# Expert stage without GpSimd arithmetic: splits on VectorE, the gate factor at the combine

## The chip, the cores and the metric

The kernel runs on one core of a Trainium2 chip. The metric is the device time of one execution in microseconds (us), the median of several runs. The engines are TensorE (PE, with its weight loads as PEld), VectorE (DVE), ScalarE (ACT), GpSimd (POOL) and SyncE (SP), whose queue issues the large loads.

## The reference, cut to what matters

Two transformer blocks on 512 tokens of width 1024, in fp32. The first has a delta rule and a sliding window, then a mixture of 32 experts of which each token takes 4; the second has attention, a recurrent layer and two MLPs. The change lies in the experts:

```python
logits = xf @ w_router + b_router
top_val, top_idx = lax.top_k(logits, 4)
gates = softmax(top_val)
# for the tokens of expert e:
hu = xb @ w_up[e] + b_up[e]                       # 1024 -> 2048
act = x_glu * sigmoid(1.702 * x_glu) * (x_lin + 1)  # both halves clipped at 7
ys = (act @ w_down[e] + b_down[e]) * row_gate     # summed by token
x = x + gate2 * moe(h)                            # gate2: one factor per column
```

## The kernel before, in words

Every fp32 weight block is turned into two parts whose products PE can take: `split` (L278 to L287) lets ACT write the rounded part `wh` (L281) and then DVE (L286) or POOL (L284) the rest, `wl = raw - wh`. `mm3` makes three products of the parts (L290 to L292), `prod` the like for blocks of 64 rows (L1168 to L1174).

Expert stage: the routing ranks the experts by their tokens. The list `units` holds 13 units of 256 rows, blocks of 128 or 64 rows of an expert. `gather_T` collects the rows of a unit by products with one-hot columns (`hot_cols`, L1083). An expert has twelve weight blocks of 128x2048, eight in `expert_up` and four in `expert_down`, each a load of 1 MB on SP's queue into one of six buffers `raw`. The list `pools` says which of the twelve POOL splits: blocks 4 and 2, more in the first unit. `expert_up` has the activation on ACT and DVE (L1204 to L1212), `split_T` the transposes. `expert_down` of an expert follows `expert_up` of the next; `expert_out` multiplies its rows by the routing gate on ACT or DVE, and its `finish` multiplies them on POOL by `g2bc`, the factor gate2 of the columns (L1262), and scatters them to `y_d` in DRAM by an indirect DMA of POOL (L1263). The buffer `yb` for this is single. `slots` (L1100 to L1111) makes the row numbers and gates of a block from a small product with the records `R`: four columns, put together by operations on one column each. The rows of the last two blocks don't pass through `y_d`: `add_rows` makes factors of a product from them (L1279 to L1281).

Combine: each token block of 128 takes the four slots of its tokens from `y_d` (`load_y`, L1550) and adds them to the residual `xs`, one addition in two on POOL (`add_ys`, L1554, L1555), and the products of the last blocks (L1573). The loads for the third and fourth token block follow the first loads of the attention's weights. Then the second block begins.

The order of each engine's instructions is not that of the source: the program is built with `schedule_with_timeline_sim=True`, which plans it from data dependences and assumed durations. An engine executes its own list in order. Of memory, a tile waits until the tile whose place it takes is no longer read.

Of the kernel before, what the change touches and what calls it, by code (L numbers as in the profile page):

```python
# [7 lines left out]
F = mybir.dt.float32  # L8
# [8 lines left out]
T = 512  # L17
# [5 lines left out]
SMALL = 18  # the experts by rank: from 2 up to 192 tokens for two of them, 64 from this one on, else 128  # L23
# [38 lines left out]
_RC, _NRC = _layout([("iota", 128), ("Us", 128), ("thi", 4), ("tlo", 4), ("p32", 1), ("d32", 1), ("eq", 32), ("kc", 32), ("cap", 32)])  # L62


def _rconst():
    import numpy as np
    c = np.zeros((128, _NRC), np.float32)

    def put(name, a):
        o, n = _RC[name]  # L70
        c[:, o:o + n] = a
    i = np.arange(128)
    put("iota", np.repeat(i[None], 128, 0))
    put("Us", i[:, None] < i[None])
    put("thi", np.arange(4)[None] * 8 + (i // 16)[:, None] - 32)
    put("tlo", np.repeat((i % 16)[:, None], 4, 1))
# [151 lines left out]
def tile_block(ctx, tc, A, out, dbg=None):  # L228
# [23 lines left out]
    # eight banks of PSUM, in groups that are used in turn  # L252
# [83 lines left out]
    def gemv(src, cofs, gp, bufs):  # L336
        """silu(c) @ src; columns 256 q .. 256 q + 255 end up in row 32 q"""
# [9 lines left out]
    def gemv_split(src, cofs, gp, ring_raw, nv=4):  # L347
        """the same, with the products and most of the sums on the other engines"""
# [35 lines left out]
    def mod_row(i, src, cofs, gp, bias, plus=0.0, mul=None, how="split"):  # L384
        """row i of md_d: (silu(c) @ src + bias + plus) * mul"""
# [82 lines left out]
    # gains and biases of the second block's norms, times sqrt(2) for the residual  # L468
# [33 lines left out]
    # gates of the delta rule  # L502
# [54 lines left out]
    def front(p):  # L557
        """doubled silu of the convolutions, inverse norms, the triangular systems"""
# [181 lines left out]
    # sliding-window attention; the logits of a head are kept in units of its slope  # L740
# [89 lines left out]
    # row slot * T + token of y_d; the last two experts' first tokens, of the slots 2 and 3, do not pass through it  # L830
# [11 lines left out]
    # output projection: the columns of the window's attention first  # L842
# [29 lines left out]
    # gated norm of the delta rule's output  # L872
# [29 lines left out]
    # residual, second norm, router  # L902
# [14 lines left out]
    # the norm's gain goes into the router's weights; the shift's share of the logits  # L917
# [18 lines left out]
    # those that are read last come first, away from the room of the experts' weights  # L936
# [7 lines left out]
    M = Z[:, :, 0:32]  # a token's chosen experts; then its gates, then its places  # L944
# [21 lines left out]
    # the experts' input bias in two parts, the columns' second half 64 rows further on  # L966
# [9 lines left out]
    def half_out(tb, ps, half):  # L976
        """half the columns of the residual, their share of its square and, before the norm's factor, of the logits"""
# [56 lines left out]
    # routing  # L1034
# [12 lines left out]
    thi = RC("thi").unsqueeze(2).to_broadcast([128, 4, 32])  # L1047
    R = mt([128, 4, 32, 4], "R")
    pool.memset(R[:, :, :, 3], 1.0)
    vec.tensor_copy(out=R[:, :, :, 1], in_=RC("tlo").unsqueeze(2).to_broadcast([128, 4, 32]))  # L1050

    # one plus a pair's place among its expert's tokens, 0 for the pairs that are not chosen
# [10 lines left out]
    # units of 256 rows; a block of rows is an expert's rank, its columns in the unit, and the places that it leaves out  # L1063
# [53 lines left out]
    def gather_T(hot, X, runs):  # L1117
        """hi and lo of the transposed rows of h2 that the one-hot columns select"""
# [14 lines left out]
    def rows_in(X, blk):  # L1133
        """the stationary operands of a block in X: hi, lo, and both side by side"""
# [44 lines left out]
    def expert_up(wsrc, bsel, rows, get=fetch):  # L1179
        """an expert's activations, in chunks of 256 of its hidden columns"""  # L1180
        acts_ = [mt([128, 1024], "ma", 2, F, mo)[0:r[0]] for r in rows]
        for j in range(4):
# [9 lines left out]
            for kh in range(2):  # L1192
                h, l = get(wsrc, 2 * j + kh, pool if 2 * j + kh in pools[0] else None)
# [21 lines left out]
    def split_T(src, to=None):  # L1215
        """the stationary operands of the transposed activations"""
# [28 lines left out]
    def gated(yb, y, gc, s):  # L1245
        """gate times 64 rows in two parts"""
# [4 lines left out]
    def expert_out(y, sl, r, yb=None):  # L1251
        """gates a block's rows; the function that it returns writes them to y_d"""
# [8 lines left out]
        def finish():  # L1261
            pool.tensor_tensor(out=yb[0:r], in0=yb[0:r], in1=g2bc[0:r], op=OP.mult)  # L1262
# [26 lines left out]
    def block_rows(blk):  # L1289
        """a block's one-hot columns, its rows of y_d and its gates"""  # L1290
# [7 lines left out]
    def ranked(rank):  # L1298
        """the weights and the bias of the expert of a rank"""
# [5 lines left out]
    def further_block(at, hot):  # L1305
# [7 lines left out]
        Rc, bs = mt([128, 4, 4], "Rc"), mt([128, 1], "bs", 1, FR)  # L1313
# [41 lines left out]
    vec.tensor_copy(out=R[:, :, :, 2], in_=z4[:, :, 32:64])  # L1355
# [16 lines left out]
    vec.scalar_tensor_tensor(out=R[:, :, :, 0], in0=jv.rearrange("p (t e) -> p t e", t=4), scalar=32.0, in1=thi,  # L1372
# [8 lines left out]
    def lists():  # L1381
        """the blocks beyond the experts' own: ranks, experts, offsets of their places, and the number of them"""
# [9 lines left out]
        # a block per partition: its rank is the number of ranks whose blocks all come before it  # L1392
# [4 lines left out]
        # places less 128 times the blocks before in the expert, less what its own hold  # L1397
# [23 lines left out]
    # experts  # L1421
# [3 lines left out]
    def begin(src, ready, ahead):  # L1425
        """the first weights of a block from what was loaded before"""
        def get(s, k, eng=None):
            if s is not src or k >= len(ahead):
                return fetch(s, k, eng)
# [3 lines left out]
            return msplit(ahead[k], eng)  # L1433
# [4 lines left out]
    def expert_bias():  # L1438
        # the residual, and the experts' output bias: hi * hi + lo * hi + hi * lo in one product
# [15 lines left out]
        for tb in range(NTB):  # L1455
# [18 lines left out]
    LOOP = 1  # the unit after which any further blocks come  # L1474
# [3 lines left out]
    for u, unit in enumerate(units):  # L1478
# [35 lines left out]
        if u == LOOP:  # L1514
            # any further blocks
# [584 lines left out]
```

## Time and profile before

| | |
|---|---|
| median of 3 runs | 3288.72 us (3272.14 to 3291.38) |
| profiled execution, span | 3273.7 us, 37859 instructions |
| PE busy | 2902.4 us, 89% |
| DVE busy | 2627.4 us, 80% |
| ACT busy | 1597.7 us, 49% |
| POOL busy | 1181.6 us, 36% |
| mean granted clock of PE | 0.947 |

The span goes from the first to the last instruction; no other time of the profiled execution is listed, and it lies within 2 us of the fastest of the runs. Busy time is that in which an instruction of the engine is open, waiting for a resource inside the instruction included. A row names the line, the engine, the operation, out<-in by the program's names and the form (partitions x elements), then the count; what stands after the second bar is idle time before the group and what ended it.

### The profile page before, as it was taken

How to read it: one execution, taken by the hardware profiler on the slowest of the kernel's cores; microseconds unless marked ns; L12 is line 12 of the kernel's file. 1: busy time of each engine (PE TensorE's matmuls, PEld its weight loads, DVE VectorE, ACT ScalarE, POOL GpSimd, SP SyncE). 2: the span in 40 equal slices, each digit the busy share in tenths (PEclk: the TensorE clock that was granted, in tenths of full speed). 3: DMA queues.
4: the chain of work that ended last, by engine and by line, in shares of the span. 5: the costliest groups of instructions: out<-in, count | busy, mean ns of one | idle time of the engine just before them, and what ended most of it. 6: DMA issues, size and time to landing. Idle time of an engine off the chain costs nothing.

```text
span 3273.7 us, 37859 instructions
## 1 busy us (share of the span) xinstructions
PE 2902.4 (89%) x13632; PEld 2225.4 (68%) x13632; DVE 2627.4 (80%) x3392; ACT 1597.7 (49%) x1960; POOL 1181.6 (36%) x531
## 2 busy tenths in 40 slices
PE   6889988888899898999989759889999889889997
PEld 4667866655677566667667537577777767678886
DVE  5986479989999999999998985686756888875456
ACT  4433344666666656666666544442223645533231
POOL 2330165334443343344434562233323243442223
PEclk9999979989999999999999879989999999989999
DMA  7552346778688778778878754345532322223321
GB/s 264 182 176 87 106 169 236 296 274 314 248 305 304 287 290 303 280 271 302 305 284 311 276 195 161 116 147 199 178 128 89 112 63 92 83 84 100 100 92 56
DMA packets 127201, 643.73 MB, mean 197 GB/s; under 512 B 17142, under 2 KB 18122, under 8 KB 77856
## 3 DMA queue, kind: packets, MB, share of 16 engines
q1 hardware_dynamic: 122064, 632.27, 53.8%
q0 software_dynamic: 4800, 8.46, 0.7%
q8 instruction: 109, 1.79, 0.2%
q14 instruction: 84, 0.69, 0.1%
q10 hardware_dynamic: 144, 0.52, 0.0%
HBM read 624.42 MB, written 21.59 MB: 197 GB/s over the span
## 4 chain that ended last, share of the span: by engine, by line
PE 38%; DVE 26%; issue 7%; ACT 4%; DMA 2%; POOL 1%; DVEq 0%; ACTq 0%; SPq 0%; POOLq 0%
DVE wl L286 9%; PE bank_d L290 4%; PE bank_d L292 4%; PE bank_d L291 4%; PE bank_u L290 3%; PE bank_u L292 3%; PE bank_u L291 3%; DVE ma L1211 3%; ACT wh L281 2%; PE bank_hu L290 2%; PE bank_hu L291 2%; PE bank_hu L292 1%; DVE ma L1208 1%; PE bank_tr L1125 1%; PE bank_hu L1173 1%
## 5 line engine op out<-in xcount | busy, mean ns | idle before, releaser
L281 ACT CAST wh<-raw 128x2048 fp32r<-128x2048 f32 (+1 forms) x615 | 958.0, 1579 | 528.5 <-PE bank_u L291 177.7
L286 DVE TENSOR_TENSOR wl<-raw,wh 128x2048 fp32r<-128x2048 f32 (+2 forms) x521 | 1065.1, 2052 | 149.0 <-ACT wh L281 147.0
L284 POOL TENSOR_TENSOR wl<-raw,wh 128x2048 fp32r<-128x2048 f32 (+1 forms) x94 | 443.0, 4715 | 659.8 <-ACT wh L281 603.1
L1682 POOL TENSOR_TENSOR h2h<-h2h,yt 128x512 f32<-128x512 f32 x161 | 237.5, 1482 | 679.5 <-DVE yt L1681 669.5
L1681 DVE TENSOR_TENSOR yt<-bank_d,G 128x512 f32<-128x512 f32 x168 | 113.2, 686 | 182.9 <-PE bank_d L292 180.1
L291 PE MATMUL bank_u<-h_lo,wh 128*128 128x512 f32 (+1 forms) x680 | 251.3, 370 | 9.8 <-DVE h_lo L1666 9.8
L290 PE MATMUL bank_u<-h_hi,wh 128*128 128x512 f32 (+1 forms) x680 | 252.2, 373 | 6.3 <-ACT wh L281 3.2
L292 PE MATMUL bank_u<-h_hi,wl 128*128 128x512 f32 (+1 forms) x680 | 251.6, 371 | 0.0
L291 PE MATMUL bank_hu<-wl,xT 128*128 128x512 f32 x576 | 236.2, 411 | 14.9 <-DVE wl L286 9.6
L290 PE MATMUL bank_hu<-wh,xT 128*128 128x512 f32 x576 | 233.5, 410 | 0.0
L292 PE MATMUL bank_hu<-wh,xT 128*128 128x512 f32 x576 | 231.4, 403 | 0.0
L1262 POOL TENSOR_TENSOR yb<-yb,g2bc 128x1024 f32<-128x1024 f32 (+1 forms) x32 | 108.9, 3404 | 282.3 <-ACT yb L1259 201.8
L1173 PE MATMUL bank_hu<-wl,xT 128*64 128x512 f32 x448 | 191.2, 427 | 21.0 <-DVE wl L286 20.6
L290 PE MATMUL bank_d<-wh,a 128*128 128x512 f32 x512 | 202.5, 396 | 5.6 <-DVE yt L1681 3.5
L291 PE MATMUL bank_d<-wl,a 128*128 128x512 f32 x512 | 200.9, 393 | 0.0
L292 PE MATMUL bank_d<-wh,b 128*128 128x512 f32 x512 | 197.5, 392 | 0.0
L1174 PE MATMUL bank_hu<-wh,xT 128*128 128x512 f32 x448 | 188.5, 421 | 0.0
L1209 ACT ACTIVATE mb<-ma 128x256 f32<-128x256 f32 (+1 forms) x136 | 56.6, 417 | 265.4 <-DVE ma L1208 245.0
L1211 DVE SCALAR_TENSOR_TENSOR ma<-mb,ma 128x256 f32<-128x256 f32 (+1 forms) x136 | 153.6, 1129 | 8.4 <-ACT mb L1209 8.2
L291 PEld LDWEIGHTS bank_u<-h_lo,wh 128*128 128x128 f32 x680 | 130.8, 192 | 32.5 <-DVE h_lo L1666 10.5
L290 PEld LDWEIGHTS bank_u<-h_hi,wh 128*128 128x128 f32 x680 | 130.6, 193 | 28.4 <-ACT wh L281 3.6
L292 PEld LDWEIGHTS bank_u<-h_hi,wl 128*128 128x128 f32 x680 | 130.7, 192 | 22.3
(626 smaller groups left out, 6572.5 us busy)
## 6 DMA issues: line engine op xcount, KB each, us to landing
raw<-in_w_up_dram SPq DMA_DIRECT2D x256, 1024.0 KB, 4.9
raw<-in_w_down_dram SPq DMA_DIRECT2D x128, 1024.0 KB, 5.1
raw<-in_mlp_w_dram SPq DMA_DIRECT2D x128, 512.0 KB, 4.4
graw<-in_ada_w_dram SPq DMA_DIRECT2D x72, 512.0 KB, 4.1
graw<-in_w_ada_dram SPq DMA_DIRECT2D x48, 512.0 KB, 4.6
raw<-in_ada_w_dram SPq DMA_DIRECT2D x24, 512.0 KB, 4.2
raw<-in_rnn_w_in_dram SPq DMA_DIRECT2D x24, 512.0 KB, 3.8
raw<-in_w_in_dram SPq DMA_DIRECT2D x22, 512.0 KB, 4.2
```

The lines of the kernel that those rows point to most:

```text
L281: act.copy(out=h, in_=r)
L284: pool.tensor_tensor(out=l, in0=r, in1=h.bitcast(F), op=OP.subtract)
L286: vec.tensor_tensor(out=l, in0=r, in1=h.bitcast(F), op=OP.subtract)
L290: pe.matmul(out=o, lhsT=lhs[0], rhs=rhs[0], start=first, stop=False)
L291: pe.matmul(out=o, lhsT=lhs[0], rhs=rhs[1], start=False, stop=False)
L292: pe.matmul(out=o, lhsT=lhs[1], rhs=rhs[0], start=False, stop=last)
L1173: pe.matmul(out=o[0:64], lhsT=hi(k), rhs=w[1], start=False, stop=False)
L1174: pe.matmul(out=o, lhsT=both(k), rhs=w[0], start=False, stop=last)
L1211: vec.scalar_tensor_tensor(out=a, in0=b, scalar=1.0, in1=a, op0=OP.add, op1=OP.mult)
L1262: pool.tensor_tensor(out=yb[0:r], in0=yb[0:r], in1=g2bc[0:r], op=OP.mult)
L1681: vec.tensor_tensor(out=t, in0=ps, in1=G[:, cs], op=OP.mult)
L1682: eng.tensor_tensor(out=xs[tb][:, cs], in0=xs[tb][:, cs], in1=t, op=OP.add)
```

## The change

In the expert stage POOL does no splits any more: all are DVE's. The factor gate2 is left out of `finish` and `add_rows`; the sum of a token's rows is multiplied by it once, at the combine, where all additions are DVE's. The records `R` have two columns instead of four (row number with its offset, half the gate), so `slots` needs two operations on the product instead of six. The one-hot columns of the four token blocks are made by one comparison with broadcast operands. The additions of the experts' output bias to the residual go to DVE. The loads of `y_d` for the second to fourth token block go into the six `raw` buffers, ahead of the attention's weights. Comments are removed too, which moves lines. Of the diff, cut to its core:

```diff
-    R = mt([128, 4, 32, 4], "R")
+    R = mt([128, 4, 32, 2], "R")
...
     def hot_cols(pos, hot):
-        for tb in range(NTB):
-            vec.tensor_scalar(out=hot[tb], in0=iob[:, 0:hot[tb].shape[1]], scalar1=pos[:, tb:tb + 1], scalar2=None,
-                              op0=OP.is_equal)
-        return hot
+        n = hot.shape[2]
+        vec.tensor_tensor(out=hot, in0=iob[:, 0:n].unsqueeze(1).to_broadcast([128, 4, n]),
+                          in1=pos.unsqueeze(2).to_broadcast([128, 4, n]), op=OP.is_equal)
+        return [hot[:, tb, :] for tb in range(NTB)]
...
     def slots(hot, Rsel):
-                pe.matmul(out=pt[o:o + n, 0:4], lhsT=hot[tb].bitcast(F), rhs=Rsel(tb), start=tb == 0, stop=tb == NTB - 1)
-        rec = mt([128, 4], "rec", 2)
-        vec.tensor_copy(out=rec, in_=pt[:, 0:4])
-        iv = mt([128, 1], "iv", 2)
-        vec.scalar_tensor_tensor(out=iv, in0=rec[:, 0:1], scalar=16.0, in1=rec[:, 1:2], op0=OP.mult, op1=OP.add)
-        pad = mt([128, 1], "pad", 2)
-        vec.tensor_scalar(out=pad, in0=rec[:, 3:4], scalar1=-8192.0, scalar2=8192.0, op0=OP.mult, op1=OP.add)
-        vec.tensor_tensor(out=iv, in0=iv, in1=pad, op=OP.add)
+                pe.matmul(out=pt[o:o + n, 0:2], lhsT=hot[tb].bitcast(F), rhs=Rsel(tb), start=tb == 0, stop=tb == NTB - 1)
         ii = mt([128, 1], "ii", 10, I32)
-        vec.tensor_copy(out=ii, in_=iv)
+        vec.tensor_scalar(out=ii, in0=pt[:, 0:1], scalar1=8192.0, scalar2=None, op0=OP.add)
         gc = mt([128, 1], "gc", 10)
-        vec.tensor_scalar(out=gc, in0=rec[:, 2:3], scalar1=0.5, scalar2=None, op0=OP.mult)
+        vec.tensor_copy(out=gc, in_=pt[:, 1:2])
...
-    pools = [(4,), (2,)]
...
-                h, l = get(wsrc, 2 * j + kh, pool if 2 * j + kh in pools[0] else None)
+                h, l = get(wsrc, 2 * j + kh)
...
-            h, l = get(wsrc, k2, pool if k2 in pools[1] else None)
+            h, l = get(wsrc, k2)
...
         def finish():
-            pool.tensor_tensor(out=yb[0:r], in0=yb[0:r], in1=g2bc[0:r], op=OP.mult)
             pool.indirect_dma_start(out=y_d, out_offset=bass.IndirectOffsetOnAxis(ap=sl[0][0:r, 0:1], axis=0),
...
     def add_rows(y, gc, hot, tiles):
-            vec.scalar_tensor_tensor(out=t, in0=y[h], scalar=gc, in1=g2bc[:, hs], op0=OP.mult, op1=OP.mult)
+            act.activation(out=t, in_=y[h], func=AF.Copy, scale=gc)
...
-    ready = {k: msplit(ahead[k], pool) for k in range(2)}
+    ready = {k: msplit(ahead[k]) for k in range(2)}
...
     def expert_bias():
-            pool.tensor_tensor(out=xs[tb], in0=xs[tb], in1=bt, op=OP.add)
+            vec.tensor_tensor(out=xs[tb], in0=xs[tb], in1=bt, op=OP.add)
...
-        pools[:] = [(1, 3, 5, 7), (0, 2)] if u == 0 else [(4,), (2,)]
-        if not nxt:
-            pools[1] = (0,)
...
-    def add_ys(y, tb):
-        for j in (0, 2):
-            pool.tensor_tensor(out=y[j], in0=y[j], in1=y[j + 1], op=OP.add)
-            vec.tensor_tensor(out=xs[tb], in0=xs[tb], in1=y[j], op=OP.add)
+    def sum_y(y):
+        for a, b in ((0, 1), (2, 3), (0, 2)):
+            vec.tensor_tensor(out=y[a], in0=y[a], in1=y[b], op=OP.add)
...
-    load_y(ys[1], 1)
-    add_ys(ys[0], 0)
+    for tb in range(1, NTB):
+        for j in range(2):
+            r = m_raw.tile([128, 2048], F, tag="raw", name="raw")
+            ys[tb] += [r[:, 0:1024], r[:, 1024:2048]]
+        load_y(ys[tb], tb)
+    sum_y(ys[0])
...
     for tb in range(NTB):
+        if tb:
+            sum_y(ys[tb])
         for h in range(2):
...
-            vec.tensor_tensor(out=xs[tb][:, hs], in0=xs[tb][:, hs], in1=o, op=OP.add)
-    add_ys(ys[1], 1)
+            vec.tensor_tensor(out=ys[tb][0][:, hs], in0=o, in1=ys[tb][0][:, hs], op=OP.add)
+        vec.tensor_tensor(out=ys[tb][0], in0=ys[tb][0], in1=g2bc, op=OP.mult)
+        vec.tensor_tensor(out=xs[tb], in0=xs[tb], in1=ys[tb][0], op=OP.add)
...
-    for tb in range(2, NTB):
-        load_y(ys[tb], tb)
...
-    for tb in range(2, NTB):
-        add_ys(ys[tb], tb)
```

## Rows read from the trace of the kernel before

**Rows 1.** Busy time by stretch: PE, PEld, DVE, ACT, POOL, clock, DMA share, GB/s
```profile
...
460.00:510.00 50.00, 37.08 (x197) 31.71 (x196) 37.85 (x54) 21.87 (x18) 33.48 (x7) 0.87 0.57 214
510.00:1860.00 1350.00, 1203.20 (x5473) 881.72 (x5473) 1281.06 (x1400) 843.29 (x747) 552.31 (x132) 0.95 0.78 288
```

**Rows 2.** Chain that ended last, 510 to 1860 us, by line
```profile
by line: DVE wl L286 17.0%; issue 13.1%; DVE ma L1211 6.6%; PE bank_hu L290 3.9%; PE bank_hu L291 3.7%; PE bank_hu L292 3.6%; DVE ma L1208 3.2%; PE bank_tr L1125 2.7%; PE bank_hu L1173 2.6%; PE bank_hu L1174 2.5%; PE bank_y L291 2.5%; PE ba
```

**Rows 3.** DVE's groups by form, 510 to 1860 us: busy us, mean ns, idle before
```profile
...
L286 DVE TENSOR_TENSOR wl<-raw,wh 128x2048 fp32r<-128x2048 f32 x297 | 724.0, 2445 | 31.8 <-ACT wh L281 31.5
L1211 DVE SCALAR_TENSOR_TENSOR ma<-mb,ma 128x256 f32<-128x256 f32 x71 | 88.6, 1248 | 0.9 <-ACT mb L1209 0.7
L1211 DVE SCALAR_TENSOR_TENSOR ma<-mb,ma 64x256 f32<-64x256 f32 x60 | 62.9, 1049 | 6.9 <-ACT mb L1209 6.8
L1208 DVE TENSOR_SCALAR ma<-ft 64x256 f32<-64x256 f32 x60 | 58.6, 976 | 0.3
L1212 DVE SCALAR_TENSOR_TENSOR ma<-ft,ma 64x256 f32<-64x256 f32 x60 | 52.1, 869 | 0.4
...
L1104 DVE SCALAR_TENSOR_TENSOR iv<-rec 128x1 f32<-128x1 f32 x34 | 36.6, 1075 | 0.2
...
L1083 DVE TENSOR_SCALAR hot<-iob,posm 128x128 fp32r<-128x128 bf16 x64 | 27.3, 486 | 0.0
L1107 DVE TENSOR_TENSOR iv<-iv,pad 128x1 f32<-128x1 f32 x34 | 26.6, 783 | 0.0
...
L1106 DVE TENSOR_SCALAR pad<-rec 128x1 f32<-128x1 f32 x34 | 4.8, 140 | 0.0
```

**Rows 4.** Single durations in that stretch: shortest, median, longest in ns
```profile
...
L286 DVE TENSOR_TENSOR wl<-raw,wh x297: 2268/2276/6474, 514.2 to 1857.6; 128x2048 fp32r<-128x2048 f32 x149
...
L1211 DVE SCALAR_TENSOR_TENSOR ma<-mb,ma x131: 402/409/5491, 512.0 to 1854.8; 128x256 f32<-128x256 f32 x71, 64x256 f32<-64x256 f32 x60
...
L1208 DVE TENSOR_SCALAR ma<-bank_hu x69: 402/410/425, 516.4 to 1789.8; 128x256 f32<-128x256 f32 x69
L1208 DVE TENSOR_SCALAR ma<-ft x60: 271/276/4610, 628.7 to 1852.2; 64x256 f32<-64x256 f32 x60
```

**Rows 5.** Order of time: POOL and DVE side by side, start and us
```profile
...
866.69 4.61 POOL L284 TENSOR_TENSOR wl<-raw,wh 128x2048 fp32r<-128x2048 f32 x1 [23.09 <-ACT wh L281]
...
866.96 4.62 DVE L1211 SCALAR_TENSOR_TENSOR ma<-mb,ma 64x256 f32<-64x256 f32 x1 [2.53 <-ACT mb L1209]
...
1432.84 5.88 POOL L1263 DMA_INDIRECT y_d<-yb,ii  x1 [0.28 <-POOL yb L1262]
...
1432.84 2.27 DVE L286 TENSOR_TENSOR wl<-raw,wh 128x2048 fp32r<-128x2048 f32 x1
```

**Rows 6.** POOL's groups by form, 510 to 1860 us
```profile
...
L284 POOL TENSOR_TENSOR wl<-raw,wh 128x2048 fp32r<-128x2048 f32 x63 | 336.8, 5347 | 489.4 <-ACT wh L281 438.1 <-DVE wl L286 18.1 <-DVE ma L1211 16.7
L1263 POOL DMA_INDIRECT y_d<-yb,ii x31 | 88.3, 2850 | 11.3 <-POOL yb L1262 7.3 <-issue 3.0 <-DVE ma L1212 0.6
L1262 POOL TENSOR_TENSOR yb<-yb,g2bc 128x1024 f32<-128x1024 f32 x18 | 57.6, 3202 | 201.8 <-ACT yb L1259 201.8
```

**Rows 7.** Order of time: two DVE operations, each alone
```profile
...
461.29 0.69 DVE L1341 TENSOR_TENSOR oh<-oh,gt 128x512 f32<-128x512 f32 x1
...
1944.66 1.21 DVE L1555 TENSOR_TENSOR h2h<-h2h,raw 128x1024 f32<-128x1024 f32 x1
```

**Rows 8.** Sums of L286, L281 over 52 stretches without POOL arithmetic; L281, 510:1860
```profile
...
sum 716.10, DVE 483.18; mean DVE 9.29
...
sum 716.10, ACT 383.45; mean ACT 7.37
...
sum 1350.00, ACT 677.62; mean ACT 677.62
```

**Rows 9.** DVE's groups by form, 1860 to 1960 us
```profile
...
L1555 DVE TENSOR_TENSOR h2h<-h2h,y 128x1024 f32<-128x1024 f32 x4 | 9.7, 2437 | 0.0
```

**Rows 10.** SP's queue, 1915 to 1940 us
```profile
...
1928.21 11.34 SPq L272 DMA_DIRECT2D raw<-in_attn_w_in_dram  x3
```

More of the change, by code (lines that the diff above doesn't have):

```diff
@@ L59, in _consts @@
     return c
-_RC, _NRC = _layout([("iota", 128), ("Us", 128), ("thi", 4), ("tlo", 4), ("p32", 1), ("d32", 1), ("eq", 32), ("kc", 32), ("cap", 32)])
+_RC, _NRC = _layout([("iota", 128), ("Us", 128), ("tok", 4), ("p32", 1), ("d32", 1), ("eq", 32), ("kc", 32), ("cap", 32)])
 def _rconst():
@@ L74, in _rconst @@
     put("Us", i[:, None] < i[None])
-    put("thi", np.arange(4)[None] * 8 + (i // 16)[:, None] - 32)
-    put("tlo", np.repeat((i % 16)[:, None], 4, 1))
+    put("tok", np.arange(4)[None] * 128 + i[:, None] - 512 - 8192)
     e = np.arange(32)
@@ L1046, in tile_block @@
     vec.tensor_scalar(out=iob, in0=RC("iota"), scalar1=1.0, scalar2=None, op0=OP.add)
-    thi = RC("thi").unsqueeze(2).to_broadcast([128, 4, 32])
-    R = mt([128, 4, 32, 4], "R")
-    pool.memset(R[:, :, :, 3], 1.0)
-    vec.tensor_copy(out=R[:, :, :, 1], in_=RC("tlo").unsqueeze(2).to_broadcast([128, 4, 32]))
+    tok = RC("tok").unsqueeze(2).to_broadcast([128, 4, 32])
+    R = mt([128, 4, 32, 2], "R")
     pp = trbank()
@@ L1080, in hot_cols @@
     def hot_cols(pos, hot):
-        for tb in range(NTB):
-            vec.tensor_scalar(out=hot[tb], in0=iob[:, 0:hot[tb].shape[1]], scalar1=pos[:, tb:tb + 1], scalar2=None,
-                              op0=OP.is_equal)
-        return hot
+        n = hot.shape[2]
+        vec.tensor_tensor(out=hot, in0=iob[:, 0:n].unsqueeze(1).to_broadcast([128, 4, n]),
+                          in1=pos.unsqueeze(2).to_broadcast([128, 4, n]), op=OP.is_equal)
+        return [hot[:, tb, :] for tb in range(NTB)]
     def hot_of(blk):
-        return [hots[-1][:, tb, blk[1]:blk[1] + blk[2]] for tb in range(NTB)]
+        return hots[-1][:, :, blk[1]:blk[1] + blk[2]]
     hot_unit()
@@ L1149, in tile_block, with msplit, fetch @@
     turn = [0]
-    def msplit(r, eng=None):
+    def msplit(r):
         ring[1:3] = rings[turn[0] % 2]
         turn[0] += 1
-        return split(r, eng)
-    def fetch(src, k, eng=None):
-        return msplit(raw(src(k)), eng)
-    pools = [(4,), (2,)]
+        return split(r)
+    def fetch(src, k):
+        return msplit(raw(src(k)))
     def prod(o, rows, k, w, first, last, then=None):
@@ L1273, in add_rows @@
             for o in (0, 64):
-                pe.matmul(out=pt[o:o + 64, tbs[tb]], lhsT=hot[tb].bitcast(F), rhs=ident, start=True, stop=True)
+                pe.matmul(out=pt[o:o + 64, tbs[tb]], lhsT=hot[:, tb, :].bitcast(F), rhs=ident, start=True, stop=True)
         act.copy(out=hotT, in_=pt)
@@ L1354, in tile_block @@
     vec.tensor_copy(out=M2, in_=z4[:, :, 0:32])
-    vec.tensor_copy(out=R[:, :, :, 2], in_=z4[:, :, 32:64])
+    vec.tensor_scalar(out=R[:, :, :, 1], in0=z4[:, :, 32:64], scalar1=0.5, scalar2=None, op0=OP.mult)
     vec.tensor_copy(out=posm, in_=z4[:, :, 64:96])
@@ L1370, in tile_block @@
                            op0=OP.mult, op1=OP.add)
-    vec.scalar_tensor_tensor(out=R[:, :, :, 0], in0=jv.rearrange("p (t e) -> p t e", t=4), scalar=32.0, in1=thi,
+    vec.scalar_tensor_tensor(out=R[:, :, :, 0], in0=jv.rearrange("p (t e) -> p t e", t=4), scalar=512.0, in1=tok,
                              op0=OP.mult, op1=OP.add)
@@ L1425, in begin, with get @@
     def begin(src, ready, ahead):
-        def get(s, k, eng=None):
+        def get(s, k):
             if s is not src or k >= len(ahead):
-                return fetch(s, k, eng)
+                return fetch(s, k)
             if k in ready:
@@ L1432, in get @@
                 return ready[k]
-            return msplit(ahead[k], eng)
+            return msplit(ahead[k])
         return get
@@ L1523, in tile_block, with loop_fetch @@
             lr = [mt([128, 1024], "aT", 3, F, mo) for _ in range(2)]
-            def loop_fetch(src, k, eng=None):
+            def loop_fetch(src, k):
                 for b, r in enumerate(lr):
@@ L1534, in tile_block @@
                 hot = mt([128, 1024], "ma", 2, FR, mo)[:, 0:512].rearrange("p (t s) -> p t s", t=4)
+                sl, wu_, wd_, bs = further_block(ds(i_, 1), hot)
                 hot = [hot[:, tb, :] for tb in range(NTB)]
-                sl, wu_, wd_, bs = further_block(ds(i_, 1), hot)
                 xd, ad = (t.rearrange("p (k c) -> p k c", k=8) for t in lx)
@@ L1550, in load_y @@
             sync.dma_start(out=t, in_=y_d[j * T + tb * 128:j * T + tb * 128 + 128, :])
-    def add_ys(y, tb):
-        for j in (0, 2):
-            pool.tensor_tensor(out=y[j], in0=y[j], in1=y[j + 1], op=OP.add)
-            vec.tensor_tensor(out=xs[tb], in0=xs[tb], in1=y[j], op=OP.add)
-    ys = [[h2_("l", j) for j in range(4)], []]
-    load_y(ys[0], 0)
-    for j in range(2):
-        r = m_raw.tile([128, 2048], F, tag="raw", name="raw")
-        ys[1] += [r[:, 0:1024], r[:, 1024:2048]]
-    load_y(ys[1], 1)
-    add_ys(ys[0], 0)
+    def sum_y(y):
+        for a, b in ((0, 1), (2, 3), (0, 2)):
+            vec.tensor_tensor(out=y[a], in0=y[a], in1=y[b], op=OP.add)
+    ys = [[h2_("l", j) for j in range(4)]] + [[] for tb in range(1, NTB)]
+    load_y(ys[0], 0)
+    for tb in range(1, NTB):
[4 more added lines that the diff above has]
+    sum_y(ys[0])
     aT = [mt([128, 8, 128], "aT", 3, FR, mo).rearrange("p a b -> p (a b)") for _ in range(2)]
@@ L1598, in tile_block @@
     sm = tc.alloc_tile_pool(name="sm", bufs=1, reuse_waits="tile")
-    yp = tc.alloc_tile_pool(name="yp", bufs=1, reuse_waits="tile")
-    ys += [[yp.tile([128, 1024], F, tag="y", name="y", bufs=8) for j in range(4)] for tb in range(2, NTB)]
     first = []
```

3 lines of the change are left out of this document (1 added, 2 removed).

## Prediction

> **What bounds the kernel now.** The span is 3273.7 us. I first cut it into stages, by the view of busy time per stretch [rows 1]. In the expert stage, 510 to 1860 us, VectorE (DVE) is busy 1281.06 of 1350 us, 94.9%; TensorE (PE) 1203.20, ScalarE (ACT) 843.29, GpSimd (POOL) 552.31. Then the chain that ended last, in that stretch [rows 2]: its largest shares are DVE's splits (L286, 17.0%) and a small product of the activation (L1211, 6.6%), which is worth looking at because 256 columns should cost little. Third, DVE's groups by form [rows 3] against the shortest, median and longest single duration [rows 4]. There the reader is to see that busy time is not work: L1211 has a median of 409 ns and a mean of 1049 to 1248; an operation on one column (L1104) has a mean of 1075 where its neighbour of the same form (L1106) has 140. The forms that read PSUM don't stretch: L1208 from the bank never passes 425 ns, from SBUF it reaches 4610.
>
> What stretches them is shown by the order of time [rows 5]: POOL's split starts at 866.69 and takes 4.61 us; the DVE product that starts at 866.96 takes 4.62 instead of 0.41 and ends 0.28 us after POOL. A scatter of POOL is another matter: under the one at 1432.84, 5.88 us long, a DVE split runs at 2.27, the median [rows 4, 5]. So it is POOL's arithmetic that holds DVE.
>
> **The sum for the expert stage.** All in DVE time, 510 to 1860 us.
>
> Removed, stalls: busy time less count times undisturbed (median) duration [rows 3, 4]. L286: 724.0 - 297 x 2.276 = 48. L1211, both forms: 88.6 + 62.9 - 131 x 0.409 = 98. L1208 from SBUF: 58.6 - 60 x 0.276 = 42. L1212 from SBUF: 52.1 - 60 x 0.409 = 28. L1104 and L1107, base 0.14 from L1106: 36.6 + 26.6 - 68 x 0.14 = 54. Together 269 (unrounded). POOL's arithmetic was 63 splits, 18 gate products of 128 rows [rows 6] and some of 64; the change takes all of it out of the stage but two small preparations of the output bias (under 4 us together). Smaller groups have stalls too, some 10 to 20 us by my reading; I leave them out of the sum and put them into the lower end.
>
> Added: 63 splits on DVE, 63 x 2.276 = 143. Four additions of the output bias, 1.21 each by an undisturbed addition of that size [rows 7]: 5. ACT's and PE's shares of a split are there already.
>
> Removed, work: a slot record loses four one-column operations. 34 records x 4 x 0.14 = 19 at most; such operations overlap when they don't depend on each other, so I take 15, with 10 as the other end. The one-hot columns: 64 pieces at 27.3 us [rows 3] become 16 operations of 128x512 with a broadcast operand; a product of that size with a broadcast took 0.69 [rows 7], so 11: 16 less. The 64-wide ones gain a little more. A price over 1 us for the new form would cost 5; it isn't likely to be below 0.6. The gate products on POOL vanish; their place in the combine is costed below. The halved records leave PE's small products as they are, which cost it nothing that a row would show.
>
> Net -269 + 143 + 5 - 15 - 16 = -152: DVE's need falls from 1281 to 1129 us.
>
> What of it comes through? Three bounds. With the idle share of today (5.1%), DVE gives 1129 / 0.949 = 1190 us, a gain of 160. PE was busy 1203 us [rows 1]; its busy time holds the tails of pipelined products, so it is no hard floor, but it is the next engine in line: gain 147. Third, the stage as it already runs where POOL does no arithmetic. I took the 52 stretches of over 9 us between two of POOL's arithmetic instructions from 600 to 1860, 716.1 us in all, and let the view sum them [rows 8]. DVE's splits fill 483.18 us there, 67.5%; at 2.276 that is 212, and 360 blocks at that pace take 1215. ACT's casts, the other half of a split, fill 383.45 us, 53.5%, against 677.6 of 1350 overall; at that pace they need 677.6 / 0.5355 = 1265, a gain of 85. In these stretches DVE catches up on casts made earlier, so the casts' pace is the careful end, and DVE with today's idle share the bold one. I take PE's 1203, which is between them and next to the splits' pace: **a gain of 147**.
>
> **What is moved around the stage.** Ahead of it, 460 to 510 us, six of POOL's splits become DVE's, 6 x 2.276 = 14 us in a stretch in which DVE is idle 12 [rows 1]; behind them in DVE's queue stands the routing (ranks, slots), and the first experts wait for that. They also stop holding it. I take nothing, with 14 us lost and 10 gained as the ends. Nothing is added to SP's queue there.
>
> Behind it, 1860 to 1940: three splits more (7 us), and the combine on DVE alone. Its eight additions (L1555), stretched to a mean of 2.4 us by POOL's in the largest group [rows 9], become 12 additions of slots, 4 multiplications with the gate factor and 4 additions: 12 more at 1.21, 15 us, against a stretch of at least 8 x 1.2 = 10 that goes. The factor's products at L1279 leave DVE's queue for ACT's. The loads of y for the third and fourth token block move ahead on SP's queue, into the six raw buffers, in front of the first attention weights. These buffers now come free only after the sums; the attention's three first loads, which were issued beside the combine from 1928 on [rows 10], may land later. If they wait for the whole combine, some 8 us show behind it; if not, DVE's freed time shows as up to 15 us less. I take 5 us less for both ends of the stage. The rest (up to 460 and from 2000 on) keeps its instructions; POOL's arithmetic there stays.
>
> Against the profiled execution, 3273.7 us of span: 3273.7 - 147 - 5 = 3122. That execution is near the fastest of the three timed runs (3272.14); the median, 3288.72, is 15 us above, and the gain is the same for it: **3137 us**.
>
> **The rivals.** *The blocks come no faster than the casts.* ACT's casts wait for PE to give weight buffers back, PE for DVE; the queue in front of DVE is what it caught up on. Then 1265, and 3288.7 - 85 - 5 = 3199. For it: the casts' pace in the quiet stretches [rows 8]. Against it: ACT is 62% busy in the stage, so nothing of its own holds it. 0.17.
>
> *Scatters hold DVE as arithmetic did.* POOL's queue keeps 31 scatters, 88.3 us [rows 6]. If they stalled DVE, 88 us would come back: 3137 + 88 = 3225. Against it the undisturbed splits under a scatter [rows 5]. 0.03.
>
> *Slower: a split waits at the head of DVE's queue.* POOL could afford to wait: its 63 splits stood 438.1 us for ACT's cast, 7.0 each [rows 6]. DVE's own waited 31.5 us for 297, 0.11 each [rows 3]. The instruction order is planned at build time; were the moved splits put as early in DVE's queue as they stood in POOL's, the activation (L1208 to L1212) would stand behind them, and PE behind that. The point from which it decides is 152 / 63 = 2.4 us per moved split; at half of POOL's wait, 3.5, it is 63 x 3.5 - 152 = 68 slower, 3357. The short waits of DVE's own splits speak against it. 0.04.
>
> *The engines run side by side.* Then POOL's share was a gift, and DVE pays for it: 143 + 5 - 31 = 117 more on an engine that is 94.9% busy, 3406. The pairs of rows at 866 speak against it. 0.02. The Trainium skill (Perfetto Trace Analysis, Optimizing Scalar/DVE Operations) says that a saturated DVE can be a reason to give work to GpSimd, which would speak against this change; it adds that the two share a port, so that it might not help. By that reservation, the trace agrees: 4.62 us for 0.41.
>
> **How the numbers follow.** The forecast has 0.74. Its own range is 3288.7 - 160 - 20 - 15 = 3094 (today's idle share, the small stalls, the best combine) to about 3190. With the casts' rival and 10 us lost at the ends the upper end is 3288.7 - 85 + 10 = 3214. From 3090 to 3215 leaves out the last three rivals and a little at both sides, under 2 in 10. About 1% is what a measurement of this kernel can tell from no change, 33 us; all but the last two rivals, and some part of what lies between, are beyond it: faster 0.92, same 0.04, slower 0.04.
>
> **What would show it.** In the profile after: in the expert stage L1211's mean at 0.41, L1104 and L1107 gone, no DVE instruction over 2.3 us but waits; POOL busy only with scatters, near 90 us; L286 at 360 instructions and about 820 us; DVE still over 90% of a stage of some 1200 us, PE's share up. It would be wrong if DVE's share fell under 85%, with idle time ended by ACT's casts: then the weights' way through ACT and PE is the bound. It would be wrong in the other sense if the means stayed stretched with POOL idle.

## Result and the profile after

The change is faster. Four executions after have a median of 3159.15 us (3158.41 to 3160.22), four before 3285.52 (3272.14 to 3291.38); the ratio is 0.9625, 95% interval 0.9606 to 0.9644, a gain of 126 us against a forecast of 152. The span of the profiled execution fell from 3273.7 to 3156.9 us.

From here on "the stage" goes from the first to the last activation of an expert (the first and the last ScalarE instruction `mb<-ma`), since these marks are found in every kernel; "the combine" goes from there to the first copy of the attention's `q` out of PSUM, "the second block" from there to the end. Busy time by stretch, first of the kernel before, then of the one after (the columns are those of [rows 1]):

```profile
500.98:1890.49 1389.51, 1229.23 (x5588) 898.48 (x5588) 1317.77 (x1436) 863.34 (x766) 573.76 (x136) 0.95 0.78 289
1890.49:1968.72 78.23, 48.88 (x188) 33.10 (x187) 66.19 (x45) 36.40 (x60) 47.16 (x19) 0.79 0.47 172
1968.72:3273.66 1304.94, 1196.25 (x5368) 958.75 (x5366) 886.12 (x1233) 498.53 (x762) 407.20 (x276) 0.96 0.34 112
```

```profile
502.80:1778.18 1275.38, 1195.25 (x5558) 887.22 (x5558) 1147.99 (x1275) 871.01 (x767) 145.84 (x34) 0.96 0.84 316
1778.18:1840.98 62.80, 46.08 (x199) 32.28 (x197) 48.15 (x47) 33.25 (x62) 19.34 (x10) 0.78 0.44 151
1840.98:3156.92 1315.94, 1199.31 (x5365) 959.09 (x5363) 880.82 (x1234) 498.20 (x763) 409.35 (x276) 0.95 0.34 111
```

The stage takes 1275.38 us instead of 1389.51, 114 less. DVE's busy time in it fell by 170, from 94.8% of it to 90.0%; PE's share rose from 88.5% to 93.7%. The combine gives 15 us more, what lies ahead loses 2, and the second block, where the change touches nothing, takes 11 more: 117 between the spans. The other 9 of the 126 are there because the profiled execution of before lay near the lowest of its runs.

DVE's groups after, in the stage, which answer to [rows 3]:

```profile
...
L285 DVE TENSOR_TENSOR wl<-raw,wh 128x2048 fp32r<-128x2048 f32 x371 | 843.2, 2281 | 77.6 <-ACT wh L280 76.1
...
L1199 DVE SCALAR_TENSOR_TENSOR ma<-mb,ma 128x256 f32<-128x256 f32 x72 | 32.1, 447 | 0.1
...
L1200 DVE SCALAR_TENSOR_TENSOR ma<-ft,ma 64x256 f32<-64x256 f32 x63 | 25.8, 410 | 0.3
L1199 DVE SCALAR_TENSOR_TENSOR ma<-mb,ma 64x256 f32<-64x256 f32 x63 | 25.8, 409 | 0.5 <-ACT mb L1197 0.5
...
L1196 DVE TENSOR_SCALAR ma<-ft 64x256 f32<-64x256 f32 x64 | 17.8, 278 | 0.3
...
L1080 DVE TENSOR_TENSOR hot<-iob,posm 128x512 fp32r<-128x512 bf16 x16 | 10.6, 680 | 0.0
...
L1099 DVE TENSOR_SCALAR ii<-bank_tr 128x1 int32<-128x1 f32 x34 | 5.0, 146 | 9.6 <-PE bank_tr L1097 9.5
L1101 DVE COPY gc<-bank_tr 128x1 f32<-128x1 f32 x34 | 4.9, 143 | 0.0
```

The lines have moved: L285 is DVE's split, L1199 the small product (before L1211), L1196 from SBUF the first clip (L1208), L1200 the last product (L1212), L1099 and L1101 what is left of a slot record (L1104, L1107 are gone), L1080 the one-hot columns. The reader is to see the means: 447 and 409 ns where they were 1248 and 1049, 278 where it was 976, and the split at 2281 where it was 2445. Its single durations, shortest, median and longest, of which [rows 4] has those of before:

```profile
...
L285 DVE TENSOR_TENSOR wl<-raw,wh x371: 2269/2279/2297, 501.1 to 1765.6; 128x2048 fp32r<-128x2048 f32 x186
```

No split is longer than 2297 ns; before, one took 6474. The waits in the stage, before and then after (who waited at which line for whom; us in total, times, longest):

```profile
...
ACT mb L1209 <- DVE ma L1208: 245.0, 84, 7.3
...
ACT wh L281 <- PE bank_hu L292: 49.1, 36, 8.0
...
DVE wl L286 <- ACT wh L281: 32.8, 29, 3.5
```

```profile
...
ACT wh L280 <- PE bank_hu L291: 135.8, 94, 5.3
DVE wl L285 <- ACT wh L280: 76.1, 63, 3.8
...
ACT wh L280 <- PE bank_y L291: 34.2, 30, 6.4
```

ACT's wait for the clip has fallen from 245.0 to 19.8 us. What is late instead is the way of the weights: ACT's cast waits for PE to release a buffer of rounded parts, 135.8 us in the row shown where it was 49.1 (212 over all of PE's products, where it was 76), and DVE's split for that cast, 76.1 of the 127 us in which DVE is idle. PE in its turn is idle for 80 us, and DVE's work ends 67 of them, its splits 19. So the wait goes round: PE, the cast, the split, PE. One operation still met arithmetic of POOL: an L1199 of 2.60 us at 1683.53, beside the preparation of the output bias. The two longest of PE's waits:

```profile
PE bank_tr L1215 <- DVE ma L1200: 15.6, 6, 9.7
PE bank_tr L1115 <- DVE xT L1120: 10.6, 5, 4.0
```

### The profile page after: what moved, and what is told of

Read it like the earlier page. It is cut to its first block, busy times and chain, and to the rows that moved or that the text cites. A ratio compares the mean times of both kernels' runs of the same rounds, so it can differ in the third digit from the quotient of the medians.

```text
span 3156.9 us, 37575 instructions
## 1 busy us (share of the span) xinstructions
PE 2873.7 (91%) x13632; PEld 2217.1 (70%) x13632; DVE 2436.7 (77%) x3237; ACT 1605.6 (51%) x1964; POOL 699.2 (22%) x414
## 5 line engine op out<-in xcount | busy, mean ns | idle before, releaser
L285 DVE TENSOR_TENSOR wl<-raw,wh 128x2048 fp32r<-128x2048 f32 (+2 forms) x593 | 1167.1, 1976 | 206.2 <-ACT wh L280 203.9
L1250 POOL DMA_INDIRECT y_d<-yb,ii x32 | 140.9, 4403 | 1112.3 <-ACT yb L1247 617.6
L290 PE MATMUL bank_u<-h_lo,wh 128*128 128x512 f32 (+1 forms) x680 | 251.6, 371 | 13.6 <-DVE h_lo L1647 13.6
L289 PE MATMUL bank_hu<-wh,xT 128*128 128x512 f32 x576 | 233.6, 408 | 5.5 <-ACT wh L280 5.5
L291 PE MATMUL bank_hu<-wh,xT 128*128 128x512 f32 x576 | 228.7, 401 | 0.0
L1161 PE MATMUL bank_hu<-wl,xT 128*64 128x512 f32 x448 | 180.9, 404 | 8.7 <-DVE wl L285 8.7
L1162 PE MATMUL bank_hu<-wh,xT 128*128 128x512 f32 x448 | 178.3, 398 | 0.0
L289 PEld LDWEIGHTS bank_hu<-wh,xT 128*128 128x128 f32 x576 | 109.9, 191 | 37.4 <-ACT wh L280 8.0
L290 PEld LDWEIGHTS bank_hu<-wl,xT 128*128 128x128 f32 x576 | 110.1, 191 | 32.3 <-DVE wl L285 5.1
L359 DVE SCALAR_TENSOR_TENSOR gacc<-graw,sc,gacc 128x1024 f32<-128x1024 f32 x67 | 95.9, 1431 | 44.2 <-DMA graw<-in_ada_w_dram 35.5
```

The source lines that it names most:

```text
L285: vec.tensor_tensor(out=l, in0=r, in1=h.bitcast(F), op=OP.subtract)
L289: pe.matmul(out=o, lhsT=lhs[0], rhs=rhs[0], start=first, stop=False)
L290: pe.matmul(out=o, lhsT=lhs[0], rhs=rhs[1], start=False, stop=False)
L291: pe.matmul(out=o, lhsT=lhs[1], rhs=rhs[0], start=False, stop=last)
L359: vec.scalar_tensor_tensor(out=acc, in0=r, scalar=w, in1=acc, op0=OP.mult, op1=OP.add)
L1161: pe.matmul(out=o[0:64], lhsT=hi(k), rhs=w[1], start=False, stop=False)
```

## The experiments

Three kernels leave work out, and their paragraphs say which; the others compute everything. Each was timed in four executions; the ratio is to the kernel before on the same chip. A row is the stage of that kernel in the view of busy time by stretch. The kernels are planned anew at build time, so that an edit also shifts the order of instructions that it doesn't touch.

**POOL's splits given back**, all else as after:

```diff
+    pools = [(4,), (2,)]
-                h, l = get(wsrc, 2 * j + kh)
+                h, l = get(wsrc, 2 * j + kh, pool if 2 * j + kh in pools[0] else None)
...
+        pools[:] = [(1, 3, 5, 7), (0, 2)] if u == 0 else [(4,), (2,)]
```

> The changed kernel, but POOL makes the same weight splits as before (72 in all); the gate factor stays at the combine. Lock theory (POOL's arithmetic holds DVE's two-input operations): DVE loses 72 splits of 2.28 us, 164 us, and gets stalls back of 3.3 to 3.8 us for each POOL split, 240 to 270 us; the expert stage grows by 60 to 95 us, so 3159 becomes 3220 to 3255. Side-by-side theory (POOL's share was a gift): DVE's need falls by 143 us, and the time falls by 50 to 100 us, to about 3080.

3220.53 us, ratio 0.9807 (0.9790 to 0.9823): 61 more than after. The stage, then DVE's groups and POOL's in it, and one pair of instructions in order of time:

```profile
505.97:1835.95 1329.98, 1215.24 (x5603) 896.74 (x5603) 1217.20 (x1208) 865.37 (x767) 421.78 (x100) 0.96 0.81 303
```

```profile
...
L285 DVE TENSOR_TENSOR wl<-raw,wh 128x2048 fp32r<-128x2048 f32 x303 | 734.3, 2432 | 56.7 <-ACT wh L280 55.7 <-PE bank_hu L1163 0.4
L1201 DVE SCALAR_TENSOR_TENSOR ma<-mb,ma 128x256 f32<-128x256 f32 x72 | 81.1, 1126 | 0.3 <-ACT mb L1199 0.3
L1198 DVE TENSOR_SCALAR ma<-ft 64x256 f32<-64x256 f32 x64 | 61.8, 965 | 0.6
L1201 DVE SCALAR_TENSOR_TENSOR ma<-mb,ma 64x256 f32<-64x256 f32 x63 | 58.3, 925 | 6.7 <-ACT mb L1199 6.6
...
L1202 DVE SCALAR_TENSOR_TENSOR ma<-ft,ma 64x256 f32<-64x256 f32 x63 | 42.7, 678 | 0.5
...
L283 POOL TENSOR_TENSOR wl<-raw,wh 128x2048 fp32r<-128x2048 f32 x66 | 351.8, 5330 | 604.9 <-ACT wh L280 486.4 <-issue 53.4 <-DVE ma L1198 29.8
```

```profile
856.04 4.62 POOL L283 TENSOR_TENSOR wl<-raw,wh 128x2048 fp32r<-128x2048 f32 x1 [25.86 <-ACT wh L280]
...
856.26 4.69 DVE L1201 SCALAR_TENSOR_TENSOR ma<-mb,ma 64x256 f32<-64x256 f32 x1 [2.53 <-ACT mb L1199]
```

The stretched means are back, and the pair shows why: the product that starts 0.22 us behind POOL's split takes 4.69 us. Busy time less count times median in these five groups: 734.3 - 303 x 2.276 = 45, 139.4 - 135 x 0.409 = 84, 61.8 - 64 x 0.276 = 44, 42.7 - 63 x 0.409 = 17, together 190 us, 2.9 for each of the 66 splits. DVE does one itself in 2.28. So POOL's split cost DVE more than it took off it, before PE and ACT are counted. The whole of DVE's busy time says so too: it rose by 69 us though 68 splits had left it, which makes 224 us of stall, 3.4 for each. The clip L1198 has a single input and is stretched as well (965 ns, median 276), so the hold is not confined to the two-input operations that the expectation names. The stage grew by 55 us, a little less than expected, and not all of that need be DVE's stall, for PE also waited 25 us for POOL's parts themselves:

```profile
PE bank_hu L1161 <- POOL wl L283: 21.1, 8, 5.5
```

**The factor back in `finish`**, as POOL's product on every block's rows (and in `add_rows`), and out of the combine:

```diff
+            pool.tensor_tensor(out=yb[0:r], in0=yb[0:r], in1=g2bc[0:r], op=OP.mult)
...
-        vec.tensor_tensor(out=ys[tb][0], in0=ys[tb][0], in1=g2bc, op=OP.mult)
```

> The changed kernel, but the gate factor is multiplied by POOL ahead of each scatter again, 32 products. Lock theory: about 1.6 us of DVE stall for each, 50 us in all, less 5 at the combine; with DVE now 90% busy a part of it is absorbed: 15 to 45 us more, 3174 to 3204. Side-by-side theory: no change within 5 us.

3185.87, ratio 0.9705 (0.9687 to 0.9723): 27 more than after.

```profile
499.76:1807.28 1307.52, 1205.48 (x5554) 889.13 (x5554) 1179.59 (x1272) 871.62 (x767) 273.44 (x66) 0.96 0.82 308
```

```profile
...
L1250 POOL TENSOR_TENSOR yb<-yb,g2bc 128x1024 f32<-128x1024 f32 x18 | 90.0, 5000 | 568.2 <-ACT yb L1247 568.2
L1250 POOL TENSOR_TENSOR yb<-yb,g2bc 64x1024 f32<-64x1024 f32 x14 | 79.7, 5690 | 447.4 <-DVE yb L1237 447.4
```

32 products on POOL cost DVE 32 us of busy time (1148 to 1180) and the stage 32, fewer than the 50 of stall that were expected. Here POOL is the one that waits: its product of 128 rows takes 5.00 us, 3.20 before [rows 6].

**The old slot records and one-hot columns**, with four columns of `R` and six operations on one column:

```diff
-    R = mt([128, 4, 32, 2], "R")
+    R = mt([128, 4, 32, 4], "R")
...
+        for tb in range(NTB):
+            vec.tensor_scalar(out=hot[:, tb, :], in0=iob[:, 0:hot.shape[2]], scalar1=pos[:, tb:tb + 1], scalar2=None,
+                              op0=OP.is_equal)
```

> The changed kernel with the old slot records (four columns, six operations) and the old one-hot columns (four operations each): 34 us more DVE work, none of it stalled. If DVE and PE share the pace, as the two kernels before showed (84 us off DVE gave 51 us of the expert stage, 147 off PE gave 82), it costs 15 to 30 us: 3174 to 3189. If PE alone paced: under 5.

3194.64, ratio 0.9742 (0.9707 to 0.9776): 35 more.

```profile
497.27:1815.74 1318.47, 1221.87 (x5618) 901.07 (x5617) 1175.82 (x1513) 881.99 (x773) 80.84 (x34) 0.96 0.82 308
```

```profile
L286 DVE TENSOR_TENSOR wl<-raw,wh 128x2048 fp32r<-128x2048 f32 x375 | 856.6, 2292 | 96.5 <-ACT wh L281 95.8
...
L1083 DVE TENSOR_SCALAR hot<-iob,posm 128x128 fp32r<-128x128 bf16 x64 | 13.6, 281 | 0.8 <-PE bank_tr L1125 0.8
...
L1104 DVE SCALAR_TENSOR_TENSOR iv<-rec 128x1 f32<-128x1 f32 x34 | 5.2, 154 | 0.1
```

DVE's busy time is 28 us higher, but 9 of that are four more splits that fall into this cut (375 against 371), so the old form costs some 19, less than the 34 expected. The means show what the same operations take without POOL's arithmetic: L1104 154 ns where it was 1075, the one-hot columns 281 where they were 486. The stage is 43 longer, and the run costs more than the 15 to 30 expected. More than the work went with the records; how much of that is the new order is not settled.

The three together give back 61 + 27 + 35 = 123 of the 126 us. That is no account of the 126: they were not shown to add up, the 61 hold some of PE's own wait for POOL, and the 35 are more than some 19 us of DVE's work would explain.

**What paces the stage now.** One kernel takes work from DVE alone, one from PE alone. The first leaves out the clip of the activation's linear half and its product:

```diff
-                vec.tensor_scalar(out=c, in0=c, scalar1=7.0, scalar2=-7.0, op0=OP.min, op1=OP.max)
...
-                vec.scalar_tensor_tensor(out=a, in0=c, scalar=1.0, in1=a, op0=OP.add, op1=OP.mult)
```

> The changed kernel; the clip of the activation's linear half and its product with the other half are left out, 100 us of DVE work in the expert stage. If PE sets the pace now: 0 to 25 us less, 3135 to 3159. If DVE still sets it: about 90 us less, 3070. If the delivery of the weights does: no change.

The second leaves out, in blocks of 128 rows, the product of the activations' rest with the rounded weights:

```diff
-            mm3(o, (hi(k), lo(k)), w, first, last)
+            pe.matmul(out=o, lhsT=hi(k), rhs=w[0], start=first, stop=False)
+            pe.matmul(out=o, lhsT=hi(k), rhs=w[1], start=False, stop=last)
```

> The changed kernel; in the experts' blocks of 128 rows the third product (rest of the activations times rounded weights) is left out, 864 products of 512 columns, some 200 us of PE time at 0.233 us each. If PE sets the pace of the expert stage now: the stage falls until DVE's 1148 us of work bind, to about 1210, 65 us less, 3095. If DVE sets it, or the delivery of the weights: within 15 us of 3159.

Measured: 3101.43, ratio 0.9449 (0.9433 to 0.9466), and 3049.73, 0.9287 (0.9272 to 0.9303). Their stages, in that order:

```profile
502.62:1727.12 1224.50, 1183.47 (x5582) 873.74 (x5582) 1064.37 (x1003) 862.24 (x767) 131.53 (x34) 0.99 0.86 325
```

```profile
489.02:1682.42 1193.40, 1048.47 (x4784) 741.22 (x4782) 1146.84 (x1281) 874.46 (x771) 184.37 (x34) 0.95 0.90 340
```

84 us off DVE shorten the stage by 51, and PE then fills 96.6% of it; 147 off PE shorten it by 82, and DVE then fills 96.1%. Each engine gives a little more than half of what is taken from it. In all the first run gained 58 us, which lies between the outcomes that its expectation names, and the second 109, more than the 65 expected; what is above the stage's share lies where nothing was left out. Neither is the bound alone: both pace the stage together, and its length lies above either's need. In the first run the clock granted to PE in the stage also rose, from 0.96 to 0.99 of full speed, and PE's busy time fell by 12 us with all its products in place; how much of the 51 comes by that is not taken apart.

**Delivery of the weights.** Every second weight block is made from the load of the one ahead of it, so half the weights are wrong and half the bytes are loaded:

```diff
+        if k % 2 == 0:
+            kept[0] = raw(src(k))
+        return msplit(kept[0])
```

> The changed kernel; of every two weight blocks of an expert only the first is loaded and both are made from it, so that the experts' traffic is halved and every other piece of work stays. Shared pace of PE and DVE: within 15 us of 3159, since the loads are ahead. Delivery theory (316 GB/s in the stage, 368 in its best 100 us, is near what it can get): at least 40 us less.

3168.31, ratio 0.9657 (0.9623 to 0.9692).

```profile
503.76:1802.28 1298.52, 1202.90 (x5586) 887.84 (x5586) 1162.81 (x1286) 876.90 (x770) 150.86 (x34) 0.96 0.46 165
```

165 GB/s instead of 316, and no gain: the loads don't hold the stage. That the same work on PE and DVE takes 23 us more in it may come from the new order or from a buffer that is held for two splits; this is not taken apart.

**The buffers.** One `raw` buffer less (five for six), and then also one buffer more for rounded parts:

```diff
-    m_raw = ring_pool("m_raw", 6)
+    m_raw = ring_pool("m_raw", 5)
...
-    rings = [[ring_pool(f"m{r}_wh", 2), ring_pool(f"m{r}_wl", 2)] for r in range(2)]
+    rings = [[ring_pool(f"m{r}_wh", 3 - r), ring_pool(f"m{r}_wl", 2)] for r in range(2)]
```

> The changed kernel with five raw buffers instead of six (the last sums take two other buffers). It is the comparison for the next kernel. Shared pace: 0 to 20 us more. Delivery theory: 30 us or more.

> The kernel with five raw buffers and five buffers for the rounded weights instead of four. ACT's casts stand some 210 us in the stage for PE to give such a buffer back. If the depth of these buffers couples PE and DVE: 15 to 40 us less than with five raw buffers and four. If only the sum of the work counts: within 8 us of it.

3169.72, ratio 0.9658 (0.9622 to 0.9693), and 3154.62, 0.9613 (0.9575 to 0.9651). Their stages:

```profile
503.25:1801.18 1297.93, 1203.55 (x5592) 883.85 (x5591) 1154.70 (x1278) 876.23 (x772) 203.98 (x34) 0.97 0.84 314
```

```profile
502.61:1788.72 1286.11, 1204.45 (x5592) 885.31 (x5591) 1152.48 (x1277) 874.02 (x772) 199.17 (x34) 0.97 0.84 316
```

The stage goes from 1297.9 to 1286.1 us by the fifth buffer of rounded parts (1275.4 with six `raw`). The intervals overlap, so this pair alone is a hint and no more.

**DVE's copies of gathered rows to ACT:**

```diff
-                    (vec.tensor_copy if part else act.copy)(
+                    act.copy(
```

> The changed kernel; the copies of the gathered rows that DVE makes from PSUM (80 of them, 35 us) go to ACT, which is 68% busy in the expert stage. Shared pace of PE and DVE: 15 to 30 us less, 3130 to 3145. If ACT's casts come late for it: no change or some us more.

3133.32, ratio 0.9548 (0.9532 to 0.9565): 26 less than after.

```profile
500.76:1766.85 1266.09, 1196.53 (x5592) 886.71 (x5591) 1121.62 (x1195) 901.63 (x850) 124.16 (x34) 0.97 0.84 318
```

80 instructions and 26 us have left DVE, but the stage is only 9 us shorter. 4 more lie in the combine, and 8 in the second block (1307.9 us, after 1315.9), where nothing was changed. So the copies account for at most some 9 to 13 of the 26, and as the second block shows, 9 in a stretch can also come from the order.

**Both of these together**, five `raw`, five buffers of rounded parts and the copies on ACT, which was meant as the better version:

> Five raw buffers, five buffers for the rounded weights, and the gathered rows' copies on ACT: if both effects add up, 3125 to 3140, under the changed kernel and the one with five and five buffers; if ACT becomes late, no better than 3155.

3119.80 (3115.57 to 3120.87), ratio 0.9502 (0.9486 to 0.9518): the fastest kernel that computes everything, 39 below after. The stage, and its waits:

```profile
499.59:1748.25 1248.66, 1193.74 (x5592) 879.78 (x5591) 1118.70 (x1195) 893.88 (x850) 122.07 (x34) 0.98 0.86 322
```

```profile
...
ACT wh L280 <- PE bank_hu L291: 72.9, 49, 5.0
DVE wl L285 <- ACT wh L280: 55.3, 43, 6.7
...
ACT wh L280 <- DMA raw<-in_w_up_dram: 29.6, 25, 2.3
```

Against the kernel with the copies alone the interval lies apart, and the stage is 17 us shorter although a `raw` buffer is gone. The wait of ACT's cast for PE is 72.9 us where it was 135.8 after; with the copies alone it was this:

```profile
ACT wh L280 <- PE bank_hu L291: 96.9, 83, 6.9
```

This points to the number of these buffers for a part of what the change left in the stage. How large a part is not settled, since each of the kernels has its own order.

**POOL back in the combine**, two of three sums of a token block:

```diff
-            vec.tensor_tensor(out=y[a], in0=y[a], in1=y[b], op=OP.add)
+            (pool if a + b != 2 else vec).tensor_tensor(out=y[a], in0=y[a], in1=y[b], op=OP.add)
```

> The changed kernel, but two of the three additions of a token's slots are POOL's at the combine, as before. Lock theory: POOL takes 2.4 us for each of 8 and holds DVE's additions meanwhile; from the last activation to the second block's first query columns, 63 us become 68 to 78; 5 to 15 us more in all. Side-by-side theory: up to 10 us less.

3156.84 (3156.16 to 3163.28), ratio 0.9619 (0.9603 to 0.9635): no difference from after, where more was expected. The combine:

```profile
...
1783.99:1850.83 66.84, 44.06 (x189) 31.37 (x188) 49.71 (x43) 33.36 (x62) 42.93 (x15) 0.74 0.39 136
```

It is 4 us longer (66.84 against 62.80), which is less than the other parts differ between kernels. POOL holds DVE here too, as the sums that DVE keeps show, first in the kernel after, then in this one:

```profile
L1539 DVE TENSOR_TENSOR raw<-raw 128x1024 f32<-128x1024 f32 x9 | 10.8, 1215 | 1.3 <-DMA raw<-y_d 1.3
```

```profile
L1539 DVE TENSOR_TENSOR raw<-raw 128x1024 f32<-128x1024 f32 x3 | 7.9, 2650 | 2.2 <-POOL raw L1539 2.2
```

Six sums of 1.2 us have left DVE, and stall has taken their place: its busy time in the combine is 49.71 us, 48.15 after. So POOL saves DVE nothing here and costs it little. DVE is idle for a quarter of the combine in both kernels; whether that room hides a part of the stall is not shown.

## Why the prediction was right, point by point

**POOL's arithmetic holds DVE, and moving it frees more than it adds.** Right, and the cause is shown by giving splits and products back one at a time. The groups named have the means that were named, but for one stalled L1199, and L1104 and L1107 are gone. DVE's busy time in the stage fell by 170 us where 152 was forecast. The rows of the stage name most of the 18. The one-hot columns of all widths went from 45.5 to 16.7 us, 29 where 16 was taken. Two operations in the lists of further blocks (L1390, L1401) went from 9.4 to 0.7; these are small groups of the kind that the sum left out.

**The added splits** cost what they should: 2.28 us each. **The slots and one-hots** have the price that was taken for the new form, 680 ns for a comparison of 128x512 against 0.69, but the 16 us were not work. The 27.3 of the old columns held stall, and without POOL's arithmetic the same 64 pieces take 13.6 us, so the new form saves 3 in work and the rest is stall that ended. It was the means that told here too, 486 ns against 281.

**What comes through** is the term that was mis-sized. The stage time was taken as PE's busy time, 1203 us, a gain of 147, so PE's idle time was put at nothing; measured are 114. PE's busy time came out near it (1195.25 in the new cut, 1229.23 before), but PE is idle for 80 us of the stage, 67 of them until DVE is done with something, since DVE at 90% and PE at 94% wait for each other in turn. The runs with work taken from one engine show this, 51 of 84 and 82 of 147; that the number of buffers has a part in it is what the runs with the fifth one point to. The term should have been PE's need over the share that it can reach beside a DVE so full, 93.7% as it turned out, which no row of before gives. The measured gain lies between the 147 and the careful end, the casts' pace, 85.

The sum missed by 26 us (126 for 152): the stage gave 33 less, both ends 9 more, the second block took back 11, and the medians lie 9 further apart than the two profiled spans. That the last three nearly cancel is luck.

**The ends.** The combine gave 15 where 5 was taken for both ends, the upper of the bounds; the stretch ahead lost 2 of the 14 that were feared. The attention's first loads are issued 42 us behind the last activation, 38 before, and `q` still comes 15 us earlier: the later place on SP's queue was hidden.

```profile
...
1820.18 1.28 SPq L271 DMA_DIRECT2D raw<-in_attn_w_in_dram  x3
```

**The second block** was to stay as it was. It took 11 us more in the profiled execution after. It lies between 1305 and 1316 us in all thirteen profiles, with nearly the same instructions, and not by what an experiment did to the stage: 1304.9 before, 1315.9 after, 1305.0 with the old slots, 1316.4 with the factor back. Its cause is open.

**The rivals.** The casts' pace (3199) was half true: its sign, DVE idle for ACT's casts, is there, and one buffer more for the rounded parts, with the copies on ACT, took time off; but its price was too high by 40 us. DVE's share stayed at 90.0%, above the 85% that was to be the sign of being wrong. The scatters do not hold DVE: POOL is busy with them for 140.9 us (some 90 were expected) and no split is stretched. A split at the head of DVE's queue waits 76.1 us for 371, 0.2 each, far below the 2.4 from which it decides. Side by side is excluded by the pair at 856.

## What to carry to other kernels

Busy time is not work on engines that exclude each other: compare each group's mean with its median before deciding what an offload saves, and count what the offload costs the engine that was to be spared (here 2.9 us of stall for 2.28 of work). When two engines are both near 90% busy and hand over through a few buffers, the stage ends above the need of either; leave idle time on both in the forecast (here 6% of the stage on PE and 10% on DVE remained, and today's 5.1% of DVE alone would have given 160 us), and try one buffer more where the waits point. Where an edit makes a planner re-order everything, a difference of some 10 us in one stretch is no evidence by itself: a block that the change doesn't touch moved by 11.

## What the runs showed of the hardware

The wait seems to go the other way too. In the kernel after, the six scatters of POOL during which DVE is idle take 0.91 to 1.11 us; the eight that take over 5 us, up to 18.8, all run beside a DVE without a gap. A busy DVE alone does not do it: the shortest, 0.90 us at 865.22, met one. Nothing waited for any of them:

```profile
...
L1250 POOL DMA_INDIRECT y_d<-yb,ii x32: 902/1850/18822, 559.4 to 1732.9; - x32
```

```profile
...
1052.95 18.82 POOL L1250 DMA_INDIRECT y_d<-yb,ii  x1 [27.81 <-ACT yb L1247]
```

From 1052.95 to 1071.77 DVE has no idle time, and most of it is splits and products with two inputs in SBUF; the mean of a scatter went from 2850 [rows 6] to 4403 ns. The Trainium skill (SBUF — State Buffer, Who interferes with whom) infers that an operation with two inputs doesn't hold the making of descriptors on GpSimd. Short one-input operations stood among the two-input ones in the scatter at 1052.95, but another has them apart:

```profile
727.16 7.25 POOL L1250 DMA_INDIRECT y_d<-yb,ii  x1 [42.70 <-DVE gc L1101]
```

```profile
726.93 6.68 DVE L285 TENSOR_TENSOR wl<-raw,wh 128x2048 fp32r<-128x2048 f32 x3
```

Until 733.54 DVE runs three splits and nothing else, and the scatter lasts to 734.41. That speaks against the inference for this indirect transfer, but it is not so each time: a scatter at 1702.64 took 2.10 us beside two splits. What decides it no run here takes apart.
